# Column width and unit order in the second MLP's first-weights stage, and operation width in the convolution, of a two-layer decoder trunk on one core

## The chip, the cores and the metric

The kernel runs on one core of one Trainium2 chip. The metric is device time in microseconds (us) of the whole program; of several runs the median is given. The engines are named TensorE (PE in the profile, its weight loads PEld), VectorE (DVE), ScalarE (ACT), GpSimd (POOL) and SyncE (SP), which only issues loads and stores.

## The reference, cut to what matters

Two layers on 1040 positions (16 meta tokens and 1024 real ones), width 1024, all in float32. Layer 0 mixes tokens by attention, layer 1 by a gated short convolution; each is followed by an MLP with 4096 hidden rows. The change touches the convolution layer and the MLPs:

```python
def rms_norm(x, g):
    y = xf * lax.rsqrt(jnp.mean(xf * xf, axis=-1, keepdims=True) + EPS)
    return (y * g)

def short_conv_mixer(h, w_in, conv_w, w_out):
    z = h @ w_in
    gate_b, gate_c, u = jnp.split(z, 3, axis=-1)
    g = gate_c * u
    y = conv_general_dilated(g, conv_w, padding=[(2, 0)], feature_group_count=D_MODEL)  # causal, width 3
    return (gate_b * y) @ w_out

def sq_relu_mlp(h, w_up, w_down):
    return jnp.square(jax.nn.relu(h @ w_up)) @ w_down

h = h + mixer(rms_norm(h, g_mix))
h = h + sq_relu_mlp(rms_norm(h, g_mlp), w_up, w_down)
```

## The kernel before, in words

Positions lie along the columns, features along the 128 partitions. After attention the kernel has five stages: the first MLP's first weights (`up` with `op1`), its second weights (`down`), the convolution's input weights (`up` with `op2`), its output weights (`down`), then the second MLP in the same two parts (`up` with `op3`, `down`). In the first MLP and the convolution an operand covers 1028 columns in two halves of 514; in the second MLP the meta tokens are no longer needed, and it covers the 1024 real columns in two halves of 512 (`Operand(3, 2, 512)`; `o.w` is the width of a half).

**Products in `up`.** A unit makes 256 output rows for all columns. Its weights are four blocks (r0 to r3: two halves of the input features by two halves of the output rows), its operand likewise, and the two-by-two block product is made from seven block products instead of eight. They are numbered 1 to 7, each from a sum or difference of weight blocks (`Weights.build`) and one of operand blocks (`Operand.add`). For float32 accuracy every number is split into two parts, and each block product is three matmuls (big by big, small by big, big by small) for each of four blocks of 128 features: 12 matmuls to one PSUM buffer (line 916).

A unit (`unit`, lines 919 to 953) holds three results A, B and C in PSUM, each for two chunks of columns, (0, h) and (h, o.w): 258 and 256 columns, or 256 and 256 in the second MLP. PSUM has eight buffers of 512 columns (`mp`, line 768). A unit thus takes six buffers, and it runs in three parts:
- part one: products 2, 1 and 5 into B, A and C (72 matmuls); then ScalarE copies A out (line 942) and VectorE subtracts B and C from it (lines 943 and 944);
- part two: products 4 and 3 are added onto B and C (48 matmuls), then `post` takes two of the four results out;
- part three: products 7 and 6 are added onto B and C (48 matmuls), then `post` takes the other two out.

Within a part the chunks follow each other, except in the first unit of a stage, which goes through the feature blocks in the outer loop. After each part `nxt` issues the making of the next unit's weights for the same part: two loads of 512 KB on SP's queue, sums on VectorE (lines 895, 898 and 901), a cast on ScalarE (line 907) and a subtraction on GpSimd or VectorE (line 908). Their pages come from a pool of 16 (`lp`), 12 of which a unit uses. Behind the first unit's part one the remaining operands are made too (`Operand.add`, lines 812 and 824, for the four feature blocks).

`post` in an MLP (lines 1078 to 1085): VectorE adds (line 1081, in part three), applies relu and the scale (line 1082), ScalarE squares (line 1084) and a store on ScalarE's queue takes the rows to memory (`hid`). The second MLP has 16 units, so 16 x 168 matmuls.

**The convolution** has 12 units in four groups of gate, value and output. The first `post` of an output unit makes y for two blocks of 128 features (lines 1126 to 1133): ScalarE scales g (line 1129), VectorE adds the two shifted terms (line 1131, twice), GpSimd multiplies by the norm's scale (line 1133), each on 1024 columns. Then VectorE takes the unit's results out (lines 1139 to 1142).

**Order.** The program is written in the order above, but a scheduler places the instructions on each engine's queue by a simulated timeline, earlier-written ones first among those that are ready; each queue then runs in order. A page or a PSUM buffer is given out when its last reader is placed, and a semaphore makes the next writer wait.

## Time and profile before

| | us |
|---|---|
| median of 3 runs | 2568.97 (2564.75 to 2579.14) |
| the profiled execution, its own time | 2568.92 |
| its span, first to last instruction | 2567.2 |
| matmuls busy | 2442.4 (95%) |
| VectorE busy | 1570.2 (61%) |
| ScalarE busy | 820.6 (32%) |
| GpSimd busy | 910.4 (35%) |

The mean granted clock of TensorE over the span is 0.982 of full speed. Busy time is the time in which an engine has an instruction under way. Matmuls overlap each other, so the duration of one says less than how many pass in a stretch. "Idle before" is the time an engine stood still before a row, with the instruction that ended the wait. A row of a timeline that says x96 stands for 96 instructions one after another.

### The profile page before, as it was taken

How to read it: one execution, taken by the hardware profiler on the slowest of the kernel's cores; microseconds unless marked ns; L12 is line 12 of the kernel's file. 1: busy time of each engine (PE TensorE's matmuls, PEld its weight loads, DVE VectorE, ACT ScalarE, POOL GpSimd, SP SyncE). 2: the span in 40 equal slices, each digit the busy share in tenths (PEclk: the TensorE clock that was granted, in tenths of full speed). 3: DMA queues.
4: the chain of work that ended last, by engine and by line, in shares of the span. 5: the costliest groups of instructions: out<-in, count | busy, mean ns of one | idle time of the engine just before them, and what ended most of it. 6: DMA issues, size and time to landing. Idle time of an engine off the chain costs nothing.

```text
span 2567.2 us, 42480 instructions
## 1 busy us (share of the span) xinstructions
PE 2442.4 (95%) x16526; PEld 2232.4 (87%) x16526; DVE 1570.2 (61%) x3117; ACT 820.6 (32%) x1723; POOL 910.4 (35%) x686
## 2 busy tenths in 40 slices
PE   7999899999977999999999979999889999999999
PEld 7877676689877999999999979998689999888889
DVE  8673677656679656554444588777685555543432
ACT  3222456644645333321000242221353333210100
POOL 6353454422313333334233124435223333342320
PEclk9999999999998999999999989999989999999999
DMA  4234545544152333363221212225223333631311
GB/s 156 80 116 134 166 124 167 155 124 129 39 192 71 112 107 100 114 217 123 75 104 69 83 50 66 67 67 197 99 84 106 100 101 114 214 128 69 115 58 66
DMA packets 174874, 286.13 MB, mean 111 GB/s; under 512 B 36745, under 2 KB 122185, under 8 KB 174673
## 3 DMA queue, kind: packets, MB, share of 16 engines
q1 hardware_dynamic: 88608, 217.86, 26.9%
q10 hardware_dynamic: 86064, 65.56, 8.0%
q8 instruction: 130, 2.13, 0.4%
q14 instruction: 72, 0.58, 0.1%
HBM read 198.45 MB, written 84.91 MB: 110 GB/s over the span
## 4 chain that ended last, share of the span: by engine, by line
PE 75%; DVE 10%; DMA 7%; issue 4%; ACT 2%; POOL 1%; ACTq 0%; SPq 0%; DVEq 0%; POOLq 0%
PE mp L72 31%; PE mp L916 26%; PE sc L72 9%; PE pq L72 3%; PE av L72 3%; PE tr L505 2%; DMA lp<-w_up 1%; DMA qk_d<-qk 1%; PE tr L439 1%; DMA op<-fop_d 1%; DVE lp L901 1%; DVE pg L812 1%; DVE lp L895 1%; DMA lp<-w_in_conv 1%; DVE pg L809 1%
## 5 line engine op out<-in xcount | busy, mean ns | idle before, releaser
L916 PE MATMUL mp<-pg,lp 128*128 128x256 f32 (+1 forms) x7320 | 897.2, 285 | 42.7 <-ACT wk L942 13.6
L916 PEld LDWEIGHTS mp<-pg,lp 128*128 128x128 f32 x7320 | 890.6, 192 | 49.8 <-ACT wk L942 14.0
L72 PE MATMUL mp<-pg,lp 128*128 128x342 f32 (+2 forms) x4416 | 813.6, 346 | 2.7 <-DVE pg L1024 1.4
L72 PEld LDWEIGHTS mp<-pg,lp 128*128 128x128 f32 x4416 | 734.4, 189 | 80.8 <-DVE pg L1024 2.2
L908 POOL TENSOR_TENSOR lp<-lp 128x512 fp32r<-128x512 f32 x216 | 307.2, 1428 | 637.4 <-ACT lp L907 594.8
L1046 DVE TENSOR_TENSOR pg<-pg,mp 128x342 f32<-128x342 f32 (+2 forms) x368 | 206.5, 570 | 360.8 <-PE mp L72 360.5
L1035 POOL TENSOR_TENSOR lp<-lp 128x1024 fp32r<-128x1024 f32 x72 | 184.3, 2560 | 443.4 <-PE mp L72 371.2
L907 ACT CAST lp<-lp 128x512 fp32r<-128x512 f32 x303 | 181.6, 618 | 417.3 <-DVE lp L895 259.7
L1023 ACT CAST pg<-pg 128x1024 fp32r<-128x1024 f32 (+1 forms) x72 | 75.8, 1053 | 519.2 <-DMA pg<-hid 482.8
L895 DVE TENSOR_TENSOR lp<-lp 128x512 f32<-128x512 f32 x86 | 85.6, 999 | 135.8 <-DMA lp<-w_up 91.2
L486 POOL TENSOR_SCALAR Sb<-Sb,ls 128x144 f32<-128x144 f32 (+7 forms) x128 | 97.6, 768 | 188.1 <-DVE ls L485 125.2
L72 PE MATMUL sc<-op 128*128 128x264 f32 (+11 forms) x600 | 140.5, 347 | 6.3 <-DMA op<-fop_d 5.6
L1084 ACT ACTIVATE wk<-wk 128x256 f32<-128x256 f32 (+1 forms) x256 | 103.6, 416 | 114.1 <-DVE wk L1082 112.1
L72 PE MATMUL sc<-wH,hgH 128*128 128x512 f32 (+5 forms) x328 | 122.3, 379 | 9.2 <-DVE wH L150 7.6
L72 PE MATMUL sc<-wH,hgL 128*128 128x512 f32 (+5 forms) x328 | 122.6, 377 | 5.8 <-DVE hgL L178 5.8
L1034 DVE CAST lp<-lp 128x1024 fp32r<-128x1024 f32 x72 | 96.2, 1337 | 44.1 <-DMA lp<-w_down 42.7
L72 PE MATMUL sc<-wL,hgH 128*128 128x512 f32 (+5 forms) x328 | 121.5, 375 | 0.0
L505 PE MATMUL tr<-ident,Sb 128*128 128x128 f32 x704 | 115.4, 279 | 2.4 <-ACT pt L511 0.8
L908 DVE TENSOR_TENSOR lp<-lp 128x512 fp32r<-128x512 f32 x87 | 80.3, 925 | 47.4 <-ACT lp L907 46.9
L1024 POOL TENSOR_TENSOR pg<-pg 128x1024 fp32r<-128x1024 f32 (+1 forms) x36 | 94.4, 2623 | 40.9 <-ACT pg L1023 40.8
L72 PEld LDWEIGHTS sc<-op 96*128 96x128 f32 (+1 forms) x600 | 93.3, 192 | 13.8 <-issue 7.4
L505 PEld LDWEIGHTS tr<-ident,Sb 128*128 128x128 f32 x704 | 82.8, 141 | 15.7 <-issue 3.8
(287 smaller groups left out, 2992.2 us busy)
## 6 DMA issues: line engine op xcount, KB each, us to landing
lp<-w_down SPq DMA_DIRECT2D x64, 512.0 KB, 4.5
lp<-w_up SPq DMA_DIRECT2D x62, 512.0 KB, 4.6
hid<-wk ACTq DMA_DIRECT2D x208, 128.0 KB, 2.5
pg<-hid SPq DMA_DIRECT2D x40, 512.0 KB, 5.1
pg<-hid SPq DMA_DIRECT2D x32, 514.0 KB, 5.3
res<-pg SPq DMA_DIRECT2D x24, 514.0 KB, 3.8
pg<-res SPq DMA_DIRECT2D x24, 514.0 KB, 5.9
lp<-w_in_conv SPq DMA_DIRECT2D x24, 512.0 KB, 4.6
```

Source lines behind the costliest of these rows:

```text
L72: T.matmul(ps, lhsT=l, rhs=r, start=first, stop=last)
L486: G.tensor_scalar(out=sb[:, :nk], in0=sb[:, :nk], scalar1=ls, scalar2=1.0, op0=ALU.mult, op1=ALU.mult)
L505: T.transpose(ps[:, P * (b - b0):P * (b - b0) + P], sb[:, P * b:P * b + P], ident)
L895: V.tensor_tensor(out=t[:, :512], in0=r0, in1=r3 if i == 1 else r1, op=ALU.add)
L907: S.copy(out=w[:, :512], in_=src)
L908: (V if i in (3, 7) else G).tensor_tensor(out=w[:, 512:], in0=src, in1=f(w)[:, :512], op=ALU.subtract)
L916: T.matmul(ps, lhsT=wt.W[i][:, y, k], rhs=o.N[k][i][:, x, c0:c1], start=start and k == 0 and n == 0, stop=k == 3 and n == 2, skip_group_ch ...
L1024: (V if m % 2 else G).tensor_tensor(out=l, in0=q, in1=f(h), op=ALU.subtract)
L1034: V.tensor_copy(out=h, in_=q)
L1035: G.tensor_tensor(out=l, in0=q, in1=f(h), op=ALU.subtract)
L1046: V.tensor_tensor(out=hT[m][:, c0:c1], in0=hT[m][:, c0:c1], in1=ps, op=ALU.add)
L1084: S.activation(out=q, in_=q, func=AF.Square)
```

## The change

In the second MLP (`o.w == 512`) a unit has one chunk of 512 columns instead of two of 256, so three PSUM buffers and 84 matmuls. `unit` stops at the end of each part, and `up` runs part one of a unit, then part three of the unit before it, then part two of the unit: two units are in flight. For the other stages `up` runs the three parts in the order of before. In all stages line 901's subtraction becomes two of 512 columns, and in the convolution the operations that make y run on 512 columns, (2, 514) and then (514, 1026), instead of 1024.

```diff
@@ -898,7 +898,9 @@
                         V.tensor_tensor(out=t[:, 512:1024], in0=r2, in1=r3, op=ALU.add)
                 elif i == 7:
                     t = new()
-                    V.tensor_tensor(out=t[:, :1024], in0=self.r[1], in1=self.r[0], op=ALU.subtract)
+                    for n in range(2):
+                        c = slice(512 * n, 512 * n + 512)
+                        V.tensor_tensor(out=t[:, c], in0=self.r[1][:, c], in1=self.r[0][:, c], op=ALU.subtract)
                     self.s[6], self.s[7] = t[:, :512], t[:, 512:1024]
                 src = {4: r3, 3: r0}.get(i)
                 if src is None:
@@ -920,22 +922,19 @@
 
 
         h = o.w // 2 + o.w // 2 % 2
-        CH = [(0, h), (h, o.w)]
+        CH = [(0, o.w)] if o.w == 512 else [(0, h), (h, o.w)]
         A, B, C = [[bank_(c1 - c0) for c0, c1 in CH] for _ in range(3)]
         t = {}
 
         def go(start, *todo):
-            todo = [[(i, ps[n], *CH[n]) for i, ps in todo] for n in range(2)]
+            todo = [[(i, ps[n], *CH[n]) for i, ps in todo] for n in range(len(CH))]
             if first:
-                products(o, wt, todo[0] + todo[1], start)
-            else:
-                for n in range(2):
+                products(o, wt, sum(todo, []), start)
+            for n in range(len(CH)):
+                if not first:
                     for x in todo[n]:
                         products(o, wt, [x], start)
-                    yield n
-            if first:
-                yield 0
-                yield 1
+                yield n
 
         for n in go(True, (2, B), (1, A), (5, C)):
             t[n] = work(CH[n][1] - CH[n][0])
@@ -943,14 +942,17 @@
             V.tensor_tensor(out=t[n], in0=t[n], in1=B[n], op=ALU.subtract)
             V.tensor_tensor(out=t[n], in0=t[n], in1=C[n], op=ALU.subtract)
         nxt(1)
+        yield
         for n in go(False, (4, B), (3, C)):
             post(1, 0, *CH[n], B[n], None)
             post(0, 1, *CH[n], C[n], None)
         nxt(2)
+        yield
         for n in go(False, (7, B), (6, C)):
             post(0, 0, *CH[n], B[n], t[n])
             post(1, 1, *CH[n], C[n], t[n])
         nxt(3)
+        yield
 
     PARTS = {1: (1, 5, 2), 2: (4, 3), 3: (7, 6)}
 
@@ -1007,8 +1009,17 @@
                 chain.prepare(n + 1, part)
             return go
 
+        last = iter(())
         for n, post in enumerate(posts):
-            unit(o, chain.wts[n], nxt(n), post, n == 0)
+            u = unit(o, chain.wts[n], nxt(n), post, n == 0)
+            next(u)
+            next(last, None)
+            next(u)
+            if o.w == 512:
+                last = u
+            else:
+                next(u)
+        next(last, None)
 
     def down(count, rows, lo, hi, chunks, o=None, chain=None):
 
@@ -1125,12 +1136,13 @@
                 if not y:
                     for n in range(2):
                         y[n] = lpage()
-                        d = y[n][:, 2:NC]
-                        S.activation(out=d, in_=g[n][:, 2:NC], func=AF.Copy, scale=cw[:, 2 * p + n, 2:3])
-                        for s in (1, 2):
-                            V.scalar_tensor_tensor(out=d, in0=g[n][:, 2 - s:NC - s], scalar=cw[:, 2 * p + n, 2 - s:3 - s],
-                                                   in1=d, op0=ALU.mult, op1=ALU.add)
-                        G.tensor_tensor(out=d, in0=d, in1=o.R[:, 2:NC], op=ALU.mult)
+                        for b, e in REAL:
+                            d = y[n][:, b:e]
+                            S.activation(out=d, in_=g[n][:, b:e], func=AF.Copy, scale=cw[:, 2 * p + n, 2:3])
+                            for s in (1, 2):
+                                V.scalar_tensor_tensor(out=d, in0=g[n][:, b - s:e - s], scalar=cw[:, 2 * p + n, 2 - s:3 - s],
+                                                       in1=d, op0=ALU.mult, op1=ALU.add)
+                            G.tensor_tensor(out=d, in0=d, in1=o.R[:, b:e], op=ALU.mult)
                 c = o.cols(half, c0, c1)
                 b, e = max(c.start, 2), min(c.stop, NC)
                 x = work(e - b)
```

## Rows read from the trace of the kernel before

**Rows 1.** Page, section 1: busy us, share, instructions.

```profile
PE 2442.4 (95%) x16526; PEld 2232.4 (87%) x16526; DVE 1570.2 (61%) x3117; ACT 820.6 (32%) x1723; POOL 910.4 (35%) x686
```

**Rows 2.** Page, section 4: chain of work that ended last, by line.

```profile
PE mp L72 31%; PE mp L916 26%; PE sc L72 9%; PE pq L72 3%; PE av L72 3%; PE tr L505 2%; DMA lp<-w_up 1%; DMA qk_d<-qk 1%; PE tr L439 1%; DMA op<-fop_d 1%; DVE lp L901 1%; DVE pg L812 1%; DVE lp L895 1%; DMA lp<-w_in_conv 1%; DVE pg L809 1%
```

**Rows 3.** Timeline, TensorE: start us, us, what, count [idle before].

```profile
1863.17 12.71 PE L916 MATMUL mp<-pg,lp 128*128 128x256 f32 x96
1879.47 11.42 PE L916 MATMUL mp<-pg,lp 128*128 128x256 f32 x72 [3.59 <-ACT wk L942]
1896.15 95.02 PE L916 MATMUL mp<-pg,lp 128*128 128x256 f32 x768 [5.27 <-DVE wk L1082]
1992.09 210.75 PE L916 MATMUL mp<-pg,lp 128*128 128x256 f32 x1752 [0.92 <-DVE wk L943]
```

**Rows 4.** Windows: length, busy PE, PEld, DVE, ACT, POOL; clock, DMA.

```profile
2000.00:2040.00 40.00, 40.00 (x336) 39.84 (x335) 23.31 (x44) 15.22 (x34) 13.40 (x11) 1.00 0.37 106
...
2000.00:2160.00 160.00, 159.86 (x1333) 158.64 (x1332) 93.86 (x176) 60.52 (x134) 53.17 (x40) 1.00 0.36 105
2240.00:2400.00 160.00, 160.00 (x684) 129.25 (x683) 72.88 (x81) 17.87 (x17) 61.25 (x24) 1.00 0.31 105
```

**Rows 5.** Waits of TensorE, 1860 to 2205 us: total us, times, longest.

```profile
PE mp L916 <- DVE wk L1082: 5.3, 1, 5.3
PE mp L916 <- ACT wk L942: 3.6, 1, 3.6
PE mp L916 <- DVE wk L943: 0.9, 1, 0.9
```

**Rows 6.** Timeline, VectorE, unit 0 of the second MLP.

```profile
1882.61 0.74 DVE L943 TENSOR_TENSOR wk<-wk,mp 128x256 f32<-128x256 f32 x2
...
1886.89 0.74 DVE L944 TENSOR_TENSOR wk<-wk,mp 128x256 f32<-128x256 f32 x2
...
1894.33 0.74 DVE L812 SCALAR_TENSOR_TENSOR pg<-wk,neg,pg 128x512 fp32r<-128x512 f32 x1
...
1895.59 0.74 DVE L1082 SCALAR_TENSOR_TENSOR wk<-mp,pg 128x256 f32<-128x256 f32 x2
```

**Rows 7.** Windows, matmuls of TensorE alone, behind the second wait.

```profile
1896.00:1900.00 4.00, 3.85 (x18) 0.50 0.19 66
1900.00:1905.00 5.00, 5.00 (x35) 0.77 0.27 94
```

**Rows 8.** Waits of TensorE, 1519 to 1763 us (the convolution).

```profile
PE mp L916 <- DVE wk L943: 7.4, 4, 2.7
PE mp L916 <- DVE wk L944: 3.3, 4, 1.7
PE mp L72 <- DVE lp L1034: 1.2, 1, 1.2
```

**Rows 9.** Timeline, VectorE, the convolution, third output unit.

```profile
1674.74 3.68 DVE L1131 SCALAR_TENSOR_TENSOR lp<-lp,cw 128x1024 f32<-128x1024 f32 x3 [0.49 <-ACT lp L1129]
...
1678.67 3.37 DVE L1131 SCALAR_TENSOR_TENSOR lp<-lp,cw 128x1024 f32<-128x1024 f32 x1
...
1683.66 3.38 DVE L901 TENSOR_TENSOR lp<-lp 128x1024 f32<-128x1024 f32 x1
1686.97 0.41 DVE L943 TENSOR_TENSOR wk<-wk,mp 128x256 f32<-128x256 f32 x1
```

**Rows 10.** Timeline, GpSimd, the same stretch.

```profile
1678.56 2.39 POOL L1133 TENSOR_TENSOR lp<-lp,pg 128x1024 f32<-128x1024 f32 x1 [6.18 <-DVE lp L1131]
...
1683.14 2.82 POOL L1133 TENSOR_TENSOR lp<-lp,pg 128x1024 f32<-128x1024 f32 x1
```

**Rows 11.** Timeline, VectorE, a later unit of the second MLP.

```profile
2071.68 0.69 DVE L895 TENSOR_TENSOR lp<-lp 128x512 f32<-128x512 f32 x1 [3.87 <-DMA lp<-w_up]
2072.28 0.41 DVE L943 TENSOR_TENSOR wk<-wk,mp 128x256 f32<-128x256 f32 x1
```

**Rows 12.** Waits of VectorE, 1908 to 2200 us.

```profile
DVE lp L895 <- DMA lp<-w_up: 35.8, 9, 5.5
```

## The prediction, made before the changed kernel was run

> **What bounds the kernel now.** I read the busy shares first: the matmul row of TensorE covers 95% of the span [rows 1]. That is a sum over stages, so the chain of waits came next. Its two largest entries are products: line 72 (attention, the second-weights stages) and line 916, the products that this change touches [rows 2]. So a gain has to come from the pitch at which products follow each other, or from a moment when TensorE waits. The timeline of TensorE over the second MLP's first-weights stage shows both [rows 3]. The stage runs from 1863.2 to 2202.8 us, 339.7 us for 96 + 72 + 768 + 1752 = 2688 products. That is 16 units of 168, and three waits stand between the groups.
>
> The pitch I read from two stretches in which TensorE never rests [rows 4]. In the stage itself 1333 products of 256 columns pass in 160 us, 120.0 ns each. In the second-weights stage behind it 684 products of 512 columns pass in 160 us, 233.9 ns each. Columns are thus nearly all of the price: 512 cost 1.95 times 256, not twice.
>
> The waits of the stage are three [rows 5]: 5.3 us on line 1082, 3.6 us on the copies of line 942, 0.9 us on line 943. All but the last lie in unit 0, where VectorE still makes the operands.
>
> **How unit 0 goes today.** There are eight PSUM buffers and a unit takes six. After unit 0's first 72 products two buffers are free, room for two groups of 12 of unit 1: the first piece of the stage has just 72 + 24 = 96 products, and the wait behind it ends with the copy that frees a buffer of unit 0 [rows 3]. The next piece is 72: 24 more of unit 1 and the 48 of unit 0's second part. Then TensorE stands for 5.3 us, because the results of that second part leave PSUM (line 1082) at 1895.6 us only, behind the operand work of line 812 in VectorE's queue. The third part may not be added onto the same buffer earlier [rows 5, 6]. After this wait the granted clock is 0.50 (1.2 GHz, the lower of its two levels) and then 0.77 on average, part at either level [rows 7].
>
> **The change part by part.**
>
> *512 columns.* A unit goes from 168 x 120.0 ns = 20.16 us to 84 x 233.9 ns = 19.65 us. Over 16 units that is 8.2 us less, all on the path, since TensorE is the engine that ends last in this stage. Bounds: 5 us if the 256-column pitch without small pauses (40 us / 336 = 119.0 ns, [rows 4]) is the fair comparison: 168 x 119.0 is 19.99 us a unit, 0.34 more than 19.65, 16 times, 8.2 us otherwise. I take 8.2, because pauses inside a unit should go with the longer cover described next.
>
> The Trainium skill (TensorE: Matmul & The Clock Gate, Back-to-back issue gap) gives a gap of columns over 2.4 GHz plus about 2.5 ns for a product seen alone. By that figure halving the count would save an estimated 3.4 us instead of 8.2, and the measured pitches are both longer than its gaps.
>
> *Two units in flight.* A unit now takes three PSUM buffers, so two units take six. Unit 1's first part needs no buffer of unit 0 at all. In unit 0 the 3.6 us wait for line 942 is therefore filled, and by the time TensorE comes to unit 0's third part it has done the whole of unit 1's first part instead of 48 of its 72 products: 24 x 120 ns = 2.9 us of work moved ahead of the wait for VectorE. What is late next is still VectorE (lines 812 and 1082), so the 5.3 us wait shrinks and doesn't vanish. I take -2.9 us. Bounds: if unit 1's subtractions (two of 512 columns) and unit 2's three sums are queued ahead of unit 0's line 1082, VectorE is later by 5 x 0.69 = 3.4 us (0.69 us is a 512-column sum in [rows 11]); if the shorter pause keeps the clock up, another 2.6 us come back (53 products in the 9 us of [rows 7], which at 120 ns take 6.4). So +3.4 to -5.5.
>
> In the later units the copy, the two subtractions and the reuse of B and C lie behind the older unit's third part, 24 x 233.9 ns = 5.6 us, where the halves of one unit gave 24 x 120 ns = 2.9 us. The 0.9 us on line 943 goes: -0.9.
>
> What is moved past the next unit's first part is the older unit's third part with its results (lines 1081, 1082, 1084 and the stores on ScalarE's queue) and the making of the next third weights (line 901, two casts, two line 908). The next unit's two loads on SP's queue, its three sums, casts and line 908 now stand ahead of these; GpSimd's queue issues no load. VectorE, ScalarE and GpSimd do not limit that stage (93.9, 60.5 and 53.2 us busy of 160, [rows 4]), so this is at nothing; TensorE's products hide it. If that cover went, it would cost the wait of the slower rival. ScalarE's stores of the hidden rows halve in number and double in size: nothing, as nobody waits for them until the next stage.
>
> *Line 901 in two halves, 44 units.* One 1024-column subtraction becomes two of 512: about 2 x 0.69 - 1.23 = 0.15 us more of VectorE each (1.23 us is line 1131 of the same width alone, below), hidden by products in both MLPs. Nothing there; in the convolution see next.
>
> *The convolution's operations.* In each of the four output units TensorE waits for lines 943 and 944: 7.4 and 3.3 us in all, and 1.2 us on line 1034 in the last, 11.9 us together [rows 8]. The reason stands in VectorE's order [rows 9]: between the small subtractions lie 1024-column operations. Line 1131 takes 3.68 / 3 = 1.23 us alone and 3.37 us while GpSimd runs line 1133 (2.4 us, [rows 10]); line 901 takes 3.38 us beside the second line 1133, and line 943, for which TensorE waits, starts the moment it ends. With halves a small subtraction waits for at most half of such an operation. I take half of one blocked operation, 3.38 / 2 = 1.7 us, at three of the four places: -5.1. Bounds: -11.9 if all the waits go; +3.0 if every half lands ahead of the subtractions (five operations that cost 0.15 us more each, four times).
>
> Sum: 8.2 + 2.9 + 0.9 + 5.1 = 17.1 us. The profiled execution took 2568.92 us (span 2567.2 and 1.7 around it), as good as equal to the median of 2568.97. So 2552. Its own range is 2546 to 2556.
>
> **The rivals.**
>
> *The blocked time is only moved: 2557.* GpSimd's line 1133 takes 2.1 us from a line 1131 beside it (3.37 against 1.23). Halving both sides leaves the sum of GpSimd's time, and what is done before line 943 may be the same work in more pieces. Then the convolution gains nothing: 2552 + 5 = 2557, and 2560 if the start gains nothing either. For it: line 943 follows directly on line 901, so only a changed order helps. The Trainium skill (SBUF — State Buffer, SBUF: two separate sides) says that port pair is held for the whole instruction and the other engine stands still; by that rule the total doesn't shrink, and these rows agree with it.
>
> *VectorE's queue head waits for weights: slower.* Today a sum of line 895 waits 3.87 us for its load, with the ready subtraction 943 behind it in the queue [rows 11]; such waits come to 35.8 us in nine, 5.5 us the longest [rows 12]. After the change the older unit's third part covers 5.6 us. Copy, one sum, two subtractions are an estimated 4 x 0.69 = 2.8 us, so a queue wait beyond 2.8 us ahead of line 943 stops TensorE. At 5.5 us in each of 15 units that is 2.7 x 15 = 40 us: 2592; from about 2 us a unit it is beyond +0.5%. Against it: the same pattern costs TensorE 0.9 us in the whole stage today, with less cover.
>
> *More than forecast: 2543.* The convolution's waits go entirely (another 6.8) and the clock stays up at the start (2.6).
>
> *It doesn't do what it says: 2561.* TensorE's order is already not the program's (unit 1 runs into unit 0), so two units in flight may change nothing but the columns: 8.2 us.
>
> **How the numbers follow.** Half a per cent, about what a measurement of this kernel can tell from no change, is 12.8 us: below 2556.1 is faster, above 2581.8 slower. Forecast 0.45, more than forecast 0.13: faster 0.58. Blocked time only moved 0.23, columns alone 0.09: same 0.32. Queue head 0.10. The range reaches from the better case to beyond the weakest gain and a small loss, 2541 to 2570, leaving out the slow rival and a tail of the good one.
>
> **What would show it.** In the changed profile: 1344 products in the stage at 232 to 235 ns; the first wait in it gone and the second near 2.5 us; no idle time on line 943 later; convolution waits on 943 and 944 near 6 us where there were 10.7. I am wrong if the 512-column pitch in this stage is above 238 ns, if a wait comes back in every unit, or if the convolution's waits stay at 10.7 with all operations halved.

## The result, and the profile after

The changed kernel takes 2546.87 us (median of 5 runs, 2542.57 to 2554.56) where the kernel before, on the same chip, took 2568.97 (5 runs, 2564.75 to 2579.14). The ratio is 0.9911, with a 95% interval of 0.9893 to 0.9928: faster, by 0.9%. The time lies 5 us below the forecast and inside its range. The profiled execution took 2543.92 us (span 2542.2), 25.0 us less than the one of before, where the sum of the prediction had 17.1. So the sum is to be looked through stage by stage.

I cut both spans at the first and the last product of line 916 (918 after the change) in each first-weights stage. The times are in us:

| stretch | before | after | difference | forecast |
|---|---|---|---|---|
| up to the first MLP | 772.05 | 772.20 | +0.2 | 0 |
| first MLP, first weights | 342.07 | 344.33 | +2.3 | 0 |
| from there to the convolution | 376.69 | 376.40 | -0.3 | 0 |
| convolution, input weights | 270.29 | 269.19 | -1.1 | -5.1 |
| from there to the second MLP | 102.07 | 97.74 | -4.3 | 0 |
| second MLP, first weights | 339.67 | 322.34 | -17.3 | -12.0 |
| second MLP, second weights, and the end | 364.36 | 360.00 | -4.4 | 0 |

The busy times of the page come first, against [rows 1]:

```profile
PE 2428.5 (96%) x15182; PEld 2162.6 (85%) x15182; DVE 1571.7 (62%) x3049; ACT 807.8 (32%) x1651; POOL 920.0 (36%) x694
```

1344 matmuls fewer, as the change has it, and 13.9 us less of busy TensorE. The span is 25.0 us shorter, so the other 11 us were time in which TensorE stood.

Five terms differ from the forecast: the second MLP gave more, the convolution gave nothing worth the name, and three stretches moved that the sum had at nothing. Now the timeline of TensorE over the second MLP's first-weights stage after the change, to be held against [rows 3] (start, us, what, count, and in brackets the idle time before):

```profile
1857.06 3.78 PE L72 MATMUL mp<-pg,ones 128*128 128x512 f32 x4 [6.11 <-DVE pg L847]
1859.86 29.23 PE L918 MATMUL mp<-pg,lp 128*128 128x512 f32 x120
1889.89 3.05 PE L918 MATMUL mp<-pg,lp 128*128 128x512 f32 x12 [0.80 <-DVE wk L943]
1896.24 277.11 PE L918 MATMUL mp<-pg,lp 128*128 128x512 f32 x1188 [3.31 <-ACT lp L909]
2173.19 3.44 PE L72 MATMUL mp<-pg,lp 128*128 128x512 f32 x14
2176.47 5.73 PE L918 MATMUL mp<-pg,lp 128*128 128x512 f32 x24
```

The reader is to see three things. The first piece is now 120 products of 512 columns, 240 of the old size, where it was 96. Of the three waits (3.59, 5.27 and 0.92 us, 9.8 together) the one on the copy is gone, and two are left, 0.80 and 3.31, together 4.1. The row puts the second down to a cast on ScalarE (line 909, 907 before), but that cast makes weights for a later unit (it follows the sum of line 895 at 1894.82 us, while the first unit's seven casts were done by 1820 us). VectorE's line 1093 (1082 before) ended just ahead of it:

```profile
1895.42 0.68 DVE L1093 SCALAR_TENSOR_TENSOR wk<-mp,pg 128x512 f32<-128x512 f32 x1
```

It ends at 1896.10, and the products start at 1896.24, 0.14 us later. Before, the first of the two of line 1082 ended at 1896.00 and the products started at 1896.15. In the kernel with the columns alone (below) the same lag stands behind that line, 0.15 us, with no cast there. So it is still VectorE that TensorE waits for. And 14 products of the following stage (line 72) now run inside the stage, ahead of its last 24: 3.3 us that lie within the marks and belong to the next row of the table.

The pitch is read from the same two windows as in [rows 4] (length, busy PE, PEld, DVE, ACT, POOL; clock, DMA):

```profile
2000.00:2160.00 160.00, 160.00 (x692) 129.79 (x691) 96.06 (x124) 55.87 (x98) 61.75 (x43) 1.00 0.37 116
2240.00:2400.00 160.00, 160.00 (x686) 129.24 (x685) 64.26 (x76) 12.62 (x12) 47.58 (x19) 1.00 0.23 79
```

In the stage 160 us / 692 = 231.2 ns, below the 233.2 ns (160 / 686) that the same width takes in the stage behind it. A unit of 84 is 19.42 us instead of 20.16, and 16 units give 11.8 us, not 8.2. (All these pitches are counts of a window, with the two or three products that reach over its edges; they are good for comparing with each other.)

With that the stage's 17.3 us come out: 11.8 by the pitch; 5.7 by the waits (9.8 to 4.1); 3.3 the other way for the 14 products of the next stage. What is left is 3.1 us, and it stands where products run below the stage's pitch: before, 339.67 less 2688 x 0.120 = 322.6 of products and 9.8 of waits leaves 7.3 us, and after, 322.34 less 1344 x 0.2312 = 310.7, 4.1 and 3.3 leaves 4.2. That is mostly the time at a low granted clock, at the stage's start and behind the waits. In the same two windows as [rows 7], which had 0.50 and 0.77, the matmuls of TensorE now show:

```profile
1896.00:1900.00 4.00, 3.75 (x11) 0.61 0.20 70
1900.00:1905.00 5.00, 5.00 (x23) 1.00 0.14 52
```

So the second window is wholly at the upper of the two levels (2.4 GHz), after a pause of 3.3 us instead of 5.3. The start of the stage thus gave 5.7 + 3.1 = 8.8 us, more than twice the 3.8 of the sum (2.9 and 0.9). The next view shows that it is the start and not the whole length: products of line 916 or 918 alone, counted from the stage's first product (length, busy, count, clock, DMA). Before:

```profile
1863.17:1923.17 60.00, 51.15 (x372) 0.87 0.26 81
1863.17:2163.17 300.00, 289.90 (x2357) 0.97 0.33 100
```

and after:

```profile
1859.86:1919.86 60.00, 55.89 (x228) 0.96 0.28 92
1859.86:2159.86 300.00, 295.89 (x1263) 0.99 0.34 108
```

After 60 us the changed kernel has done 2 x 228 = 456 products of the old size, 84 more than before; after 300 us 2526, 169 more. At 120 ns these are 10.1 and 20.3 us: half of the lead is made in the first fifth of the stage.

The convolution is the term that failed. The waits of TensorE in it after the change, against [rows 8] (total us, times, longest):

```profile
PE mp L918 <- DVE wk L942: 7.0, 4, 3.2
PE mp L918 <- DVE wk L943: 2.7, 2, 1.4
PE mp L918 <- DVE wk L1154: 1.5, 2, 1.1
```

These are the waits behind the long one at the stage's start (7.5 us, before and after). They come to 11.2 us where they were 11.9. Lines 942, 943 and 1154 are 943, 944 and 1142 of before; the longest wait has grown from 2.7 to 3.2 us. VectorE's and GpSimd's order in the third output unit shows why, and answers to [rows 9] and [rows 10]. VectorE after the change (line 1143 is 1131 before, 903 is 901):

```profile
1676.58 5.10 DVE L1143 SCALAR_TENSOR_TENSOR lp<-lp,cw 128x512 f32<-128x512 f32 x6
1681.61 0.41 DVE L942 TENSOR_TENSOR wk<-wk,mp 128x258 f32<-128x258 f32 x1
1681.94 3.13 DVE L1143 SCALAR_TENSOR_TENSOR lp<-lp,cw 128x512 f32<-128x512 f32 x2
1685.00 0.41 DVE L943 TENSOR_TENSOR wk<-wk,mp 128x258 f32<-128x258 f32 x1
...
1686.68 2.38 DVE L903 TENSOR_TENSOR lp<-lp 128x512 f32<-128x512 f32 x2
1688.98 0.41 DVE L942 TENSOR_TENSOR wk<-wk,mp 128x256 f32<-128x256 f32 x1
```

and GpSimd in the same stretch (line 1145 is 1133 before):

```profile
1678.81 1.67 POOL L1145 TENSOR_TENSOR lp<-lp,pg 128x512 f32<-128x512 f32 x1 [4.15 <-DVE lp L1143]
1681.10 1.74 POOL L1145 TENSOR_TENSOR lp<-lp,pg 128x512 f32<-128x512 f32 x1 [0.63 <-DVE lp L1143]
1682.79 1.74 POOL L910 TENSOR_TENSOR lp<-lp 128x512 fp32r<-128x512 f32 x1
1684.49 3.42 POOL L1145 TENSOR_TENSOR lp<-lp,pg 128x512 f32<-128x512 f32 x2
```

Before, three of line 1131 stood ahead of the first small subtraction, 3.68 us; now there are six halves in one row, 5.10 us, with GpSimd's first half beside them. The two halves behind it take 3.13 us, where one alone takes 0.74, since GpSimd's second half and then its line 910 run beside them. The pieces are smaller, but the same ones stand ahead of the same subtraction. And GpSimd has become slower: the halves take 1.7 us each, four of them 6.83 us, where two whole ones took 2.39 and 2.82, 5.21 together. Over the stretch from 1519 to 1763 us the groups of instructions say the same (count, then busy us and mean ns, then idle time before). Before:

```profile
L1133 POOL TENSOR_TENSOR lp<-lp,pg 128x1024 f32<-128x1024 f32 x8 | 20.4, 2555 | 28.9 <-DVE lp L1131 14.8 <-PE mp L916 14.2
```

and after:

```profile
L1145 POOL TENSOR_TENSOR lp<-lp,pg 128x512 f32<-128x512 f32 x16 | 27.0, 1696 | 28.2 <-DVE lp L1143 28.2
```

27.0 us instead of 20.4 for the same elements.

Of the stretches with no term in the sum, the one ahead of the second MLP moved most. TensorE waits there for line 847: 11.09 us before, 6.11 after (the first row of the timeline above). VectorE's four of line 847 begin at the same point and end 3.2 us apart. Before:

```profile
1855.23 5.69 DVE L847 TENSOR_TENSOR pg<-pg,wk 128x512 f32<-128x512 f32 x4
```

and after, first VectorE, then GpSimd beside it:

```profile
1855.11 2.50 DVE L847 TENSOR_TENSOR pg<-pg,wk 128x512 f32<-128x512 f32 x4
```

```profile
1855.15 9.27 POOL L910 TENSOR_TENSOR lp<-lp 128x512 fp32r<-128x512 f32 x4 [34.32 <-ACT lp L909]
```

After the change VectorE came first by 0.04 us, its four ran back to back, and GpSimd's four took 9.27 us, the first of them 4.2. Before, GpSimd's first began 0.09 us ahead of VectorE's (at 1855.14), and VectorE's four took the longer time. Whether this belongs to the change is looked at below.

### The profile page after: what moved, and what is told of

It reads as the page before. It is cut to its first block, busy times and chain, and to the rows that moved or that the text cites. A ratio compares the mean times of both kernels' runs of the same rounds, so it can differ in the third digit from the quotient of the medians.

```text
span 2542.2 us, 39452 instructions
## 1 busy us (share of the span) xinstructions
PE 2428.5 (96%) x15182; PEld 2162.6 (85%) x15182; DVE 1571.7 (62%) x3049; ACT 807.8 (32%) x1651; POOL 920.0 (36%) x694
## 4 chain that ended last, share of the span: by engine, by line
PE 79%; DVE 9%; DMA 6%; issue 4%; ACT 1%; POOL 1%; SPq 0%; ACTq 0%; DVEq 0%; POOLq 0%
PE mp L72 32%; PE mp L918 29%; PE sc L72 8%; PE pq L72 3%; PE av L72 3%; PE tr L505 3%; DVE lp L1143 1%; DMA qk_d<-qk 1%; DMA lp<-w_in_conv 1%; PE tr L439 1%; DMA lp<-w_up 1%; DVE hgL L178 1%; DVE pg L812 0%; DVE pg L809 0%; PE tr L333 0%
## 5 line engine op out<-in xcount | busy, mean ns | idle before, releaser
L918 PE MATMUL mp<-pg,lp 128*128 128x256 f32 (+2 forms) x5976 | 882.6, 310 | 39.9 <-ACT wk L941 10.7
L918 PEld LDWEIGHTS mp<-pg,lp 128*128 128x128 f32 x5976 | 818.1, 191 | 104.6 <-ACT wk L941 10.9
L72 PEld LDWEIGHTS mp<-pg,lp 128*128 128x128 f32 x4416 | 734.8, 189 | 77.8 <-DVE pg L1035 1.0
L895 DVE TENSOR_TENSOR lp<-lp 128x512 f32<-128x512 f32 x86 | 72.4, 846 | 124.1 <-DMA lp<-w_up 84.3
L1095 ACT ACTIVATE wk<-wk 128x258 f32<-128x258 f32 (+1 forms) x192 | 92.3, 488 | 116.0 <-DVE wk L1093 106.5
L1045 DVE CAST lp<-lp 128x1024 fp32r<-128x1024 f32 x72 | 97.0, 1347 | 33.9 <-DMA lp<-w_down 30.5
```

The lines of the kernel that those rows point to most:

```text
L72: T.matmul(ps, lhsT=l, rhs=r, start=first, stop=last)
L918: T.matmul(ps, lhsT=wt.W[i][:, y, k], rhs=o.N[k][i][:, x, c0:c1], start=start and k == 0 and n == 0, stop=k == 3 and n == 2, skip_group_ch ...
L1045: V.tensor_copy(out=h, in_=q)
L1095: S.activation(out=q, in_=q, func=AF.Square)
```

## The experiments

Each run lists its median, its ratio to the kernel before on the same chip with the 95% interval, and, where a stage decides, the time between the marks of the table. Diffs are against the kernel before, unless another is named.

**The second MLP's part, in two steps.** The question is which of the two carries the gain, the columns or the order of the units. The first run has the 512 columns alone, one unit after the other, with line 901 and the convolution as before. It is the kernel of the second run below with this difference:

```diff
             next(u)
             next(last, None)
             next(u)
-            if o.w == 512:
-                last = u
-            else:
-                next(u)
+            next(u)
         next(last, None)
```

> 512 columns in the second MLP, units one after another as before, all other operations on 1024 columns. Theory (the column price and the scheduler's own run-ahead do it): with three buffers a unit, the next unit's part one is pulled forward by the scheduler anyway, so the stage takes 322 to 328 us from its first product to its last, products at 232 to 234 ns, no wait over 1 us in the later units; time about 2548 to 2554. Rival (the explicit order of two units is what makes it work): part two waits for copy and subtractions in each unit, some 2 us each, 15 times, stage above 345 us and no gain over before.

Measured: 2545.37 us, 0.9934 [0.9915, 0.9952]. The second run has columns and two units in flight, with line 901 and the convolution as before:

```diff
-        CH = [(0, h), (h, o.w)]
+        CH = [(0, o.w)] if o.w == 512 else [(0, h), (h, o.w)]
...
+            next(u)
+            next(last, None)
+            next(u)
+            if o.w == 512:
+                last = u
+            else:
+                next(u)
+        next(last, None)
```

> 512 columns and two units in flight, without the halved operations. Theory (the gain of the change lies in the second MLP alone): stage 320 to 324 us, ratio to before 0.991 to 0.993, as the whole change or a little better, because the first MLP's start keeps its 342.1 us instead of 344.3. Rival (the halved operations carry part of the gain): 2552 or more, and the 4.3 us that the changed kernel saves between the convolution's products and the second MLP's first product are not there.

Measured: 2537.31 us, 0.9907 [0.9890, 0.9923]. With the columns alone, the second MLP's two stages (in that kernel the products of both mix at the border, so they are taken together, up to the last product) take 683.21 us, with two in flight 679.37, before 700.69. Two units in flight are thus worth some 4 us of 21 between these two. The seven profiled executions of this study with two in flight and eight buffers lie between 678.9 and 681.4 us, so it is rather 2 to 4, with a single execution on the other side; the intervals of the two ratios overlap. That it isn't more is explained by the timeline of TensorE in the kernel with the columns alone (the last row is cut at 1960 us, as in the two timelines further below):

```profile
1856.67 29.67 PE L916 MATMUL mp<-pg,lp 128*128 128x512 f32 x120
1889.77 4.62 PE L916 MATMUL mp<-pg,lp 128*128 128x512 f32 x12 [3.43 <-DVE wk L941]
1894.86 5.80 PE L916 MATMUL mp<-pg,lp 128*128 128x512 f32 x24 [0.47 <-DVE wk L1088]
1901.05 59.32 PE L916 MATMUL mp<-pg,lp 128*128 128x512 f32 x254 [0.40 <-ACT lp L907]
```

The first piece is 120 here too, and no wait follows until 2155 us. The program's order asks for unit 0's three parts one after another, and TensorE runs ahead of it all the same, as it did before the change; three buffers a unit are what lets it. So the start is gained by the narrower use of PSUM, which comes with the 512 columns, and not by the order of the parts.

The second of these kernels is the whole change without its halves, and it isn't slower than the change (0.9907 against 0.9911). The halves together give nothing that these runs can tell.

**The halves, one by one.** First line 901 alone:

```diff
-                    V.tensor_tensor(out=t[:, :1024], in0=self.r[1], in1=self.r[0], op=ALU.subtract)
+                    for n in range(2):
+                        c = slice(512 * n, 512 * n + 512)
+                        V.tensor_tensor(out=t[:, c], in0=self.r[1][:, c], in1=self.r[0][:, c], op=ALU.subtract)
```

> Line 901's subtraction in two halves of 512 alone. Theory: VectorE's extra 0.15 us a unit is hidden by products, so no change but at the start of the first MLP, where VectorE is late: that stage 342 to 345 us, total between 0 and 3 us slower. Rival: halves let small operations through, the convolution's waits fall from 11.9 to below 8 us and the kernel is 3 us or more faster.

Measured: 2566.72 us, 1.0019 [1.0009, 1.0028]. A small loss: the first MLP's stage takes 344.75 us (342.07 before), the convolution 272.96 (270.29 before, 268.7 to 271.2 in the four kernels with all its operations whole). Then the convolution's y alone:

```diff
-                        d = y[n][:, 2:NC]
...
-                        G.tensor_tensor(out=d, in0=d, in1=o.R[:, 2:NC], op=ALU.mult)
+                        for b, e in REAL:
+                            d = y[n][:, b:e]
...
+                            G.tensor_tensor(out=d, in0=d, in1=o.R[:, b:e], op=ALU.mult)
```

> The convolution's y in halves of 512 alone. Theory (the blocked time is only moved): TensorE's waits on lines 943 and 944 of the convolution stay at 9 to 12 us, the stage at 268 to 271 us, total within 3 us of before. Rival (the forecast's term): waits near 6 us, total about 5 us faster.

Measured: 2560.07 us, 0.9989 [0.9980, 0.9999]. The convolution takes 268.96 us. Its waits, without the first one, which stands ahead of the stage's work in all kernels:

```profile
PE mp L916 <- DVE wk L943: 5.6, 4, 1.7
PE mp L916 <- DVE wk L944: 4.1, 3, 1.4
PE mp L916 <- DVE wk L1143: 2.1, 3, 1.1
```

11.8 us, as before: some of the wait on 943 has gone to 944 and to the results, and the sum stays. Then the change with line 901 whole again:

```diff
-                    for n in range(2):
-                        c = slice(512 * n, 512 * n + 512)
-                        V.tensor_tensor(out=t[:, c], in0=self.r[1][:, c], in1=self.r[0][:, c], op=ALU.subtract)
+                    V.tensor_tensor(out=t[:, :1024], in0=self.r[1], in1=self.r[0], op=ALU.subtract)
```

> The whole change but with line 901's subtraction left on 1024 columns (512 columns, two units in flight, the convolution's halves). Theory (halves of line 901 cost at the first MLP's start and in the convolution, gain at most 3 us in the second MLP): first MLP's stage back to 341 to 342.5 us, total 2 to 5 us below the changed kernel, ratio near 0.990. Rival (the halves belong to the gain): 2 us or more above the changed kernel.

Measured: 2540.90 us, 0.9913 [0.9899, 0.9927], against 0.9911 for the change: the same. The first MLP is back at 341.45 us. The convolution takes 266.51 us, but the kernel with y's halves alone has the same convolution and took 268.96, so 2.5 us there are spread. The last of this group has two units in flight and the halves of line 901 in the second MLP alone, none in the convolution:

```diff
-              Chain([a["w_up1"][u] for u in range(DFF // P // 2)])]
+              Chain([a["w_up1"][u] for u in range(DFF // P // 2)], 512)]
```

> 512 columns and two units in flight, line 901 in halves in the second MLP's units alone, the convolution's operations whole. Theory: first MLP's stage as before (341 to 342.5 us), convolution 268 to 271 us, second MLP's two stages 677 to 680 us together; total as e2_cols_flight within 2 us. Rival (halves shorten the second MLP's start): two stages under 676 us together, total 3 us or more below e2_cols_flight.

Measured: 2542.86 us, 0.9925 [0.9912, 0.9938]. The second MLP's stage takes 324.73 us where whole subtractions took 322.75 and 324.38. Line 901's halves help in none of the three stages. In the first MLP the stage is at 344.33 and 344.75 us in the two kernels with halves there, and at 341.07 to 342.07 in all ten profiled executions with whole subtractions there and eight PSUM buffers. The loss lies at the stage's start: the second unit's line 901 (903 in halves) stands there in VectorE's queue beside GpSimd's line 908. Before, and then with the halves alone:

```profile
774.33 1.99 DVE L901 TENSOR_TENSOR lp<-lp 128x1024 f32<-128x1024 f32 x1
773.34 3.15 DVE L903 TENSOR_TENSOR lp<-lp 128x512 f32<-128x512 f32 x2
```

So the halves cost 1.2 us more here, not 0.15. The first products also come about 1 us earlier with the halves (TensorE's wait for line 847 ahead of them is 5.6 us, not 6.6), and that by itself lengthens the stage by these marks, not the program; how the rest divides isn't shown.

**What holds the convolution.** If GpSimd's multiply takes the time from VectorE, then that multiply on VectorE itself must free TensorE, though VectorE gets more to do. The kernel with two units in flight and whole operations, with this:

```diff
-                        G.tensor_tensor(out=d, in0=d, in1=o.R[:, 2:NC], op=ALU.mult)
+                        V.tensor_tensor(out=d, in0=d, in1=o.R[:, 2:NC], op=ALU.mult)
```

> As e2_cols_flight, but line 1133's multiplication of y runs on VectorE instead of GpSimd. Theory (a two-input operation of VectorE stands still while GpSimd works, 2.1 us per line 1133): VectorE takes on 2 x 1.23 us per output unit and loses 2 x 2.1 us of standing, line 1131 is 1.2 to 1.3 us everywhere, TensorE's waits on the two subtractions fall from 9.1 to 4 to 7 us. Rival (the long operations are long for another reason, such as their own reads): line 1131 keeps a longest of 3.3 us and the waits grow by 2 us per output unit.

Measured: 2524.22 us, 0.9851 [0.9837, 0.9865], the fastest of all; the convolution takes 257.81 us instead of 268.67. Its waits behind the first:

```profile
PE mp L916 <- DVE wk L941: 0.5, 1, 0.5
PE mp L916 <- DVE wk L940: 0.5, 1, 0.5
```

1.0 us is left of 11.9; on the two subtractions 4 to 7 had been expected. VectorE in the third output unit of a second execution of this kernel (lines 1140 and 1142 are 1131 and 1133, 940 and 941 are 943 and 944):

```profile
1665.13 3.68 DVE L1140 SCALAR_TENSOR_TENSOR lp<-lp,cw 128x1024 f32<-128x1024 f32 x3 [0.50 <-ACT lp L1138]
1668.72 0.42 DVE L940 TENSOR_TENSOR wk<-wk,mp 128x258 f32<-128x258 f32 x1
1669.06 1.28 DVE L1140 SCALAR_TENSOR_TENSOR lp<-lp,cw 128x1024 f32<-128x1024 f32 x1
1670.26 1.22 DVE L1142 TENSOR_TENSOR lp<-lp,pg 128x1024 f32<-128x1024 f32 x1
1671.39 0.42 DVE L941 TENSOR_TENSOR wk<-wk,mp 128x258 f32<-128x258 f32 x1
```

The fourth of line 1131 takes 1.28 us where it took 3.37 [rows 9], and the multiply, 2.4 to 2.8 us on GpSimd [rows 10], takes 1.22 here. Both together are shorter than the one operation was beside GpSimd. So VectorE's queue became shorter by taking on work. The operations are still 1024 columns wide: width was not what held TensorE.

To see it without the second MLP's change, the same one line in the kernel before:

> The kernel before with line 1133's multiplication on VectorE and nothing else. Theory (the convolution's waits come from GpSimd's share of the port, and are independent of the second MLP's order): convolution 257 to 260 us where it was 269 to 271, total 10 to 14 us below before, ratio 0.9945 to 0.9960. Rival (it needs the new order): under 5 us.

Measured: 2543.87 us, 0.9936 [0.9912, 0.9959], and the convolution at 258.45 us. One word in one line takes 11.8 us from the convolution, near half of what the whole change gives. Its second MLP, which is the program of before, took 335.62 + 359.80 = 695.4 us; the same program took 700.7 in the kernel before and 699.4 with the convolution's halves alone. That spread bears on the main term too. In the window of [rows 4] this execution has

```profile
2000.00:2160.00 160.00, 160.00 (x1347) 160.00 (x1346) 98.28 (x174) 58.97 (x130) 56.28 (x39) 1.00 0.37 110
```

160 us / 1347 = 118.8 ns for 256 columns, where the execution of before had 120.0. Against this one the change's first-weights stage is 13.3 us shorter, not 17.3, and the pitch gives 8.6 us (16 x (168 x 0.1188 - 84 x 0.2312)), not 11.8. Some 3 to 4 us of the gain by the table are thus pauses that the narrow program has in one execution and not in another.

**How far TensorE runs ahead.** The theory is that the free PSUM buffers set it. A unit takes three now; eight buffers leave five, five leave two. The kernel with two units in flight and whole operations, with

```diff
-    mp = ctx.enter_context(tc.tile_pool(name="mp", bufs=8, space=PSUM))
+    mp = ctx.enter_context(tc.tile_pool(name="mp", bufs=5, space=PSUM))
```

> As e2_cols_flight with five PSUM buffers instead of eight. It tests what the buffers are worth at the start and later. Theory (the start gains because unit 1's first part needs no buffer of unit 0): with five, only two are free after unit 0's first part, a wait of 1 to 4 us on the copy of A comes back in the second MLP's start, the stages of the second MLP together are 2 to 6 us longer than in e2_cols_flight, and the later units show no waits. Rival (run-ahead of the scheduler in all units carries the stage): waits of 1 us or more in most of the units, 15 us or more longer; the first MLP and the convolution, which want six buffers a unit, are much longer in either case and are not compared.

Measured: 2556.72 us, 0.9979 [0.9967, 0.9992]. The pool serves other stages too, and the first MLP (+4.5 us against eight buffers) and the convolution (+6.3) lose with it; the second MLP's stage takes 329.65 us instead of 322.75. Its timeline:

```profile
1868.56 15.88 PE L916 MATMUL mp<-pg,lp 128*128 128x512 f32 x60
1885.38 3.06 PE L916 MATMUL mp<-pg,lp 128*128 128x512 f32 x12 [0.94 <-ACT wk L939]
1892.45 4.40 PE L916 MATMUL mp<-pg,lp 128*128 128x512 f32 x12 [4.00 <-DVE wk L940]
1899.43 60.76 PE L916 MATMUL mp<-pg,lp 128*128 128x512 f32 x248 [2.58 <-DVE wk L941]
```

60 is unit 0's 36 and two groups of 12 for two free buffers. The next 12 wait for the copy that frees one of unit 0's, and the 12 behind them for a subtraction. The waits are 7.5 us together, with no other wait in the stage. The stage is 6.9 us longer than with eight, which is most of the 8.8 us that the start gave; both stages together are 7.0 us longer, where 2 to 6 were expected. With six buffers, in a single run:

```diff
-    mp = ctx.enter_context(tc.tile_pool(name="mp", bufs=8, space=PSUM))
+    mp = ctx.enter_context(tc.tile_pool(name="mp", bufs=6, space=PSUM))
```

> As e2_cols_flight with six PSUM buffers instead of eight, so that three are free behind unit 0's first part, just what unit 1's first part takes: the run-ahead that the forecast counted. Theory (free buffers set how much is done ahead of the start's waits): the first piece has about 72 products (36 + 36) before a wait on the copy of A, and the second MLP's first stage lies between those with five and with eight buffers, 325 to 329 us by the same marks (322.75 with eight, 329.65 with five). Rival (buffers beyond unit 1's part are worth nothing): 323 us, as with eight.

Measured: 2550.34 us beside 2561.5 for the kernel before; the stage takes 324.70 us, and its timeline is

```profile
1863.44 24.32 PE L916 MATMUL mp<-pg,lp 128*128 128x512 f32 x96
1891.56 5.49 PE L916 MATMUL mp<-pg,lp 128*128 128x512 f32 x12 [3.80 <-DVE wk L941]
1897.59 62.74 PE L916 MATMUL mp<-pg,lp 128*128 128x512 f32 x269 [0.55 <-ACT wk L939]
```

The first piece is 96, not the 72 that were expected: the copy on ScalarE freed a buffer in time, and unit 2 began in it. So 60, 96 and 120 products with five, six and eight buffers: the count of buffers sets the run-ahead. It doesn't set the time in the same measure. 24 more products ahead (six to eight) is 5.5 us of work, and the stage is 2 us shorter, inside the 321.5 to 324.7 of the kernels with eight and two units in flight.

**The wait ahead of the second MLP.** Is VectorE's line 847 held up by GpSimd's line 908, and would moving these for the first unit of each stage shorten the wait? The fastest kernel with

```diff
-                (V if i in (3, 7) else G).tensor_tensor(out=w[:, 512:], in0=src, in1=f(w)[:, :512], op=ALU.subtract)
+                (V if i in (3, 7) or self.head else G).tensor_tensor(out=w[:, 512:], in0=src, in1=f(w)[:, :512], op=ALU.subtract)
```

where `head` is true for a stage's first unit:

> As e7_y_on_vector, and in the first unit of each of the three first-weights stages line 908 runs on VectorE, so that GpSimd doesn't hold the port while VectorE makes the operands. Theory (the starts lose time by the same blocking: four of line 847 took 5.7 us where they take 2.5 free of it): the wait ahead of the second MLP falls from 8 to 4 to 6 us and the total by 2 to 6 us against e7. Rival (VectorE is the late engine there and every further operation on it is paid): five times 0.69 us more in each start, total 3 to 8 us slower than e7.

Measured: 2527.93 us, 0.9861 [0.9846, 0.9876]. Beside it ran the fastest kernel once more:

> The same kernel as e7_y_on_vector, timed in more rounds: ratio 0.983 to 0.987, every stage within 2 us of the first time.

Measured: 2529.95 us, 0.9870 [0.9854, 0.9887], so its gain stands in a second measurement, and the two can't be told apart. (This second execution is 6.2 us of span longer than the first; the part ahead of the first MLP alone is 7.2 us longer, so not every stage was within the 2 us that were expected.)

The edit missed the operations it was meant for. The first unit's weights are made some 40 us earlier; its line 908 ran on VectorE from 1793 to 1801 us. What runs beside line 847 belongs to the second unit and stayed on GpSimd:

```profile
1836.73 6.69 POOL L908 TENSOR_TENSOR lp<-lp 128x512 fp32r<-128x512 f32 x4 [48.71 <-ACT lp L907]
```

VectorE's four of line 847 began at 1836.58 us there and took 5.71 us, and TensorE's wait was 8.20; in the run without the edit they were 6.77 and 9.56. So this run doesn't test the theory. The second unit's line 908 would have to move, and no run has that. The traces speak for the theory all the same: one operation of line 847 takes 0.69 us in the changed kernel, where it isn't interrupted, and about 1.75 us in the others while line 908 runs. How many of the four are held differs between two executions of one kernel (5.71 and 6.77 us), and being first doesn't decide it: where they took 5.71 us in the first execution of the fastest kernel, VectorE was ahead by 0.22 us. The changed kernel's execution is the only one of the 14 with 2.50 us and a wait of 6.1; the others waited 8.0 to 11.1. The stretch takes 97.6 to 102.1 us over all kernels of this study. Whether the 4.3 us belong to the change or to that execution stays open.

## Why the prediction was right, and where not

The direction, the stage and the mechanism of the main term were right. The sum was 8 us short, and several of its terms were off in both directions.

- **512 columns: right in kind, mis-sized.** The step took the pitch of the second-weights stage, 233.9 ns, for this one. Measured 231.2 ns: 11.8 us instead of 8.2. Neither bound that I gave held it, since both used the 233.9. Why the same width goes 1% faster here isn't shown. The other side of the sum, 120.0 ns, holds some pauses: with 118.8 ns, as in one execution of the same program, it would have been 8.6 us.
- **The start of the second MLP: mis-sized by more than two.** The step counted 24 old-sized products of unit 1 as moved ahead of the wait. In fact the three buffers of a unit leave five free, and TensorE takes unit 2's part one as well: 132 products (264 old ones) before unit 0's third part against 168, so 96 more, 24 of unit 1 and 72 of unit 2. The work done in that time went from 168 x 0.120 = 20.2 to 132 x 0.2312 = 30.5 us, 10.4 more. The step's lower bound had VectorE later by 3.4 us for five operations queued ahead. The amount came, as the third part begins 36.4 us after the stage's first product instead of 33.0 (1896.24 - 1859.86, against 1896.15 - 1863.17), but by luck: unit 1's subtractions did not stand ahead of line 1093. Ahead of it came line 901's two halves and one sum more, 1.9 us together, and the rest is mostly operations that ran longer (seven above 1 us instead of four). 10.4 - 3.4 = 7.0 net; 0.9 from the last wait and about as much from the shorter time at a low clock behind the second wait, which I had named as a bound, make up the 8.8. I had counted buffers for unit 1 and stopped there.
- **"What is late next is still VectorE (lines 812 and 1082)": right.** The wait ahead of the third part has 3.3 us, not 2.5, and the products start 0.14 us behind line 1093, though the row names a cast on ScalarE. The wait on the copy went as forecast; 0.8 us on a subtraction (line 943, 944 before) came in its place.
- **Two units in flight** I had made the cause of the start's gain. The kernel with columns alone has the same first piece of 120 and 0.9934 to 0.9907. The cause is the width, by way of PSUM; the order gives 2 to 4 us, at the edge of what these runs tell.
- **The convolution: the step failed.** "A small subtraction waits for at most half of such an operation" supposes that an order with a subtraction between the halves comes about. It didn't: the halves stand in a row ahead of it. The rival of blocked time only moved was right for this term, and the waits stayed at 11.2 us of 11.9 (those on the two subtractions at 9.7 of 10.7, where the prediction wanted 6 and called 10.7 a sign of being wrong). It was even too mild: GpSimd's time grew from 20.4 to 27.0 us. By the Trainium skill (SBUF — State Buffer, SBUF: two separate sides) a GpSimd operation and a VectorE operation with two SBUF inputs exclude each other for the whole instruction. The runs agree with it: with the multiply on VectorE the operation beside it fell from 3.37 to 1.28 us and the waits from 11.9 to 1.0.
- **Line 901 at nothing: wrong by 2 to 3 us.** It was "hidden by products in both MLPs". At the first MLP's start VectorE is late and products don't hide it, and beside GpSimd the two halves took 3.15 us instead of 1.99, not 0.15 more.
- **The slower rival fell.** VectorE's queue head does wait for weights, 35.2 us in 12 times, 4.9 the longest (35.8 in 9, 5.5, in [rows 12]), but no wait of TensorE is left between 1900 and 2173 us. That the older unit's third part is what covers it isn't shown: the kernel with the columns alone, which has no such order written in, has no wait between 1901 and 2155 us either.
- **Not in the sum:** the 4.3 us ahead of the second MLP, left open above, and about 1 us behind it (4.4 less the 3.3 of the 14 products).

The parts come to 24.9: 11.8 by pitch, 8.8 at the start, 1.1 in the convolution, 4.3 ahead of the second MLP and 1.2 in the other stretches (the 14 products set off), less 2.3 in the first MLP. So the total was close in part by luck: two gains were put too low while two other terms were put too favourably, and some of what was not in the sum is spread between executions.

The version to keep is the change without its halves and with line 1133 on VectorE: 0.9851 and 0.9870 in two measurements, against 0.9911 for the change.

## What to carry to other kernels

Where the operands of a stage's first unit are still being made, count the free PSUM buffers and follow them to the end: they say how much later work TensorE can do in the meantime, and wider products that need fewer buffers gain there as well as by their pitch. Where an operation takes twice its usual time beside another engine's, cutting both in pieces moves the loss about and can lengthen it; put the two on one engine and look at the queue again, for it may become shorter. And when a change has several parts, run each alone: here one part carried nearly everything, and another was a small loss under it. Where a row names the end of a wait, look which unit that operation works for; and look in the trace whether an edit moved the operations it was meant to move.

## What the runs showed of the hardware that was not expected

GpSimd's multiply of two SBUF operands took 2.56 us on average for 1024 columns and 1.70 us for 512, in the same place: two halves cost 3.4 us. (VectorE's work beside it was in halves too.) The same multiply mostly took 1.22 us on VectorE, 1.45 on average.

VectorE's busy time counts the time in which it is held up. From 1519 to 1763 us it was busy for 192.91 us before. With the multiply on VectorE it was busy for 195.12 us, with eight operations more (11.5 us together), in a stretch that then reaches some 12 us further into the work behind. The sixteen of line 1131 alone, which are the same work, went from 29.3 to 21.0 us. A busy share thus doesn't say how much work an engine has.

By the counts of the two windows, products of 512 columns followed each other at 231.2 ns in the first-weights stage and at 233.2 ns in the second-weights stage, both at the full clock and with TensorE never idle. What makes the 1% wasn't tried.
